# Dense experts of the second layer: product with v laid out by token rows, weighted u part stationary, two PSUM banks for u

## The chip, the cores and the metric

The program runs on one core of one Trainium2 chip. The metric is the device time of one execution in microseconds (us). Engines are called as in the profile: PE (matrix products), DVE (vector engine), ACT (scalar engine), POOL (GpSimd), SP (the engine whose queue issues most DMAs).

## The reference, cut to what matters

A two-layer backbone: each layer mixes tokens (attention, chunk MLP, Fourier), and then every token asks 8 heads x 16 experts out of 16384. Only the second half of the second layer is touched by the change:

```python
def block(t):                                            # 128 tokens
    q = rms_unit((t @ w_q).reshape(T, PEER_HEADS, 2, PEER_HALF))
    s = jnp.einsum('thpc,hpkc->thpk', q, sub_keys)
    ...                                                  # idx: 8 x 16 experts of a token, g: their softmax weights
    act = jax.nn.gelu(jnp.einsum('td,thkd->thk', t, u_tab[idx]))
    return jnp.einsum('thk,thkd->td', g * act, v_tab[idx])
x = x + mod[:, 5] * peer_ffn(h2, ...)                    # 512 latent tokens, 1024 channels
```

## The kernel before, in words

**Dense and gathered token blocks.** The 512 latent tokens are four blocks of 128. For some blocks all 16384 experts are evaluated densely and weighted by a table that is zero where a token did not choose an expert; for the others the chosen rows of u and v are gathered. `NDBS = (4, 3)`: layer 1 has four dense blocks (TD = 512 columns), layer 2 has three (TD = 384) and one gathered block.

**The dense loop.** The experts go by in 128 chunks of 128. All factors are split into a high and a low part, so a product is three matmuls (`mm3`, L111: H x H, H x L, L x H).
- The u part of a chunk (`dense_u`, L930): the chunk's u tile is loaded (wraw), split (ACT makes wH, POOL makes wL), and 24 matmuls of TD columns fill one PSUM bank (du); ACT takes it out through Gelu (gS).
- The v part (`dense_v`, L944): the v tile is loaded (vr), ACT copies its high part (vH), DVE subtracts for the low part (vL). DVE multiplies gS by the routing weights (L964); ACT and DVE split that into AH and AL (L967). Then eight blocks of 128 channels, three matmuls each, with vH or vL stationary and AH or AL (TD columns) moving. Seven blocks accumulate in seven PSUM banks over all chunks (da_0 to da_6). The eighth goes into the eighth bank (tile d7, tag "s") and DVE adds it to an array in SBUF (L980, tile da_7).
- The du tile of the dense phase has the tag "s" too, with one buffer: u parts and d7 take turns in one bank. Before the phase, beside the routing, u parts use another pool.

**What sets the order.** The loop is written chunk by chunk; `between()` (L1226) writes the next u part ahead of the v matmuls, one for each chunk that is not "spilled". u parts run ahead: 40 chunks (c % 3 == 2, c below 120) have their gS written to DRAM early and read back into gSr (L959, two buffers); 30 more stay in SBUF. So u parts end before chunk 85, and the last 43 chunks (85 to 127) have v parts alone. Each engine runs its instructions in a fixed order, which a scheduler of the programming layer chooses from the written program by its own estimate of durations. The programmer's only hold on it is `issue_after`: L963 orders the multiplication of chunk c (gS or gSr by gt) behind the addition (L980) of chunk c - 2.

**Loads.** SP issues the loads in order: vr (512 KB, three buffers), wraw (512 KB), gSr (192 KB, one in three chunks, two buffers), and gt, the routing weights of eight chunks (1536 KB, two buffers, L950). A load into a buffer waits until the last reader of the tile that held it before.

**Gathered block.** A step asks for one row per token (POOL, L838) and three steps later uses it on DVE (L857 for u, L866 for v). Steps are spread over the matmul columns by `pace`. The rows land in four buffers.

**The end.** After the last chunk DVE adds modulation and residual channel block by channel block from PSUM (L1237 to L1245). The gathered block's result is loaded as token rows and transposed on PE, four 128x128 per bank (`residual`, L876); the scheduler interleaves the two banks, and DVE reads each transposed block (L888).

Of the kernel before, what the change touches and what calls it, by code (L numbers as in the profile page):

```python
# [10 lines left out]
F32 = mybir.dt.float32  # L11
F32R = mybir.dt.float32r
# [3 lines left out]
AF = mybir.ActivationFunctionType  # L16
# [14 lines left out]
CAND = 112         # pairs of best keys that can be among the 16 best  # L31
NK = 128
NDBS = (4, 3)      # latent token blocks whose experts are evaluated densely, per layer
OBB = 3            # buffers of the one-hot rows
XB = 2             # steps of adaLN before each of the first two norms
XA = (4, 4)        # and before the loads of each of the inputs
GP = ("px", "px")  # PSUM tags of the routing-weight table
BRE = "dve"        # engines: split of the mixers' results,
YS = "dve"         # split of the merged mixers,
ADDE = "dve"       # sums of the mixers  # L40
OB = ("PADD", "AADD") # engines of the one-hot rows of four tokens, in turns
PQB = (2, 2)       # buffers of the query weights of the routing: split, and as loaded
PQC = None         # and of the context
US = ("alt", "alt") # engine that splits the expert tables beside the routing, per layer
GT = 16            # tokens per group of the routing-weight table
NCG = 8            # chunks of experts per read of that table
TILE = 1800        # ns to load a weight tile
STEPS = ((1700, 1700, 1700), (1700, 1700, 1700)) # ns between two steps of the gathered experts: mixers, dense experts
LAG = 3            # steps from a gathered product to its sum
NGSS = (16, 30)    # chunks of experts by which u runs ahead of v, per layer  # L50
SPILL = ((40, 3), (40, 3)) # chunks whose u part goes to DRAM early, one in so many, per layer
FILL = (1.0, 1.3)  # steps of u and adaLN per step of the routing
LEAD = 2           # of which so many after the routing
ADA = 6            # adaLN column groups of the next layer beside its predecessor's routing
WBUFS = ((3, 2), (3, 4)) # buffers of weight tiles: split, and as loaded, per layer
FB = (1, 2)        # buffers of the Fourier matrices, per layer
PE2 = ("alt", "dve") # engines that split the weights of the projections, per layer
PE3 = ("dve", "dve") # and of q, k and v
ME = ("alt", "pool") # engines that split the weights of the merge beside the attention, per layer
CR = 1.75          # steps of the routing of the context per step of the last merge  # L60
CR2 = 1            # and per step of the routing of the latents
GATES = (0.5, 0.6) # steps of the gates per step of the Fourier and chunk mixers, per layer
ATT = (3, 1)       # steps of the merge per step of the attention, per layer
AN = (0.1, 0.2)    # and per step of the second norm
AD = (0.25, 0.3)   # steps of adaLN per step of the Fourier and chunk mixers, per layer

# tile numbers of the packed projection weights
# [6 lines left out]
PBANKS = {"ps": 4, "px": 2, "tl": 1, "fl": 1}     # PSUM banks of the projections  # L74
RBANKS = {"ps": 3, "px": 2, "tl": 2, "fl": 1}     # and from the attention on


class Ker:
# [19 lines left out]
    def split(self, H, L, src, h="act", l="dve"):  # L98
        """src = H + L, H with float32r's significant bits, L the exact rest."""
        nc = self.nc  # L100
        if h == "act":
            nc.scalar.activation(H, src, AF.Copy)  # L102
        else:
            nc.vector.tensor_copy(H, src)
        if l == "alt":          # both in turns
            self.turn = not self.turn
            l = "dve" if self.turn else "pool"
        e = nc.vector if l == "dve" else nc.gpsimd
        e.tensor_tensor(L, src, H.bitcast(F32), op=ALU.subtract)  # L109
# [8 lines left out]
    def mm3pair(self, out, qH, qL, kH, kL, h, qs):  # L118
        """the two halves of a head's 128 rows, on the two row tiles of the array."""
# [6 lines left out]
    def hilo(self, src, l="dve", own=None):  # L126
        """a [128, 1024] weight tile from DRAM, in two float32r parts; own: (pool, buffers of the parts, and as loaded)."""
# [17 lines left out]
    def interleave(*threads, until=None):  # L145
        """emits generators in turns, each (generator, steps per turn); all, or until one ends."""
# [19 lines left out]
    def rstd(self, tmp, r, v, scale, shape, tag, bufs=1, eps=None):  # L166
        """r = (v * scale + eps) ** -0.5: Newton steps from the guess that halves the exponent."""
# [16 lines left out]
    def setup(self):  # L184
# [9 lines left out]
        self.csil = cp.tile([P, KD, 4], F32R, name="csilr")      # high parts of both vectors, then low parts  # L194
# [13 lines left out]
    def setup_rest(self):  # L208
# [7 lines left out]
        for l, v in enumerate(self.lay):  # L216
# [11 lines left out]
            nc.vector.tensor_tensor(v["lam"], e[:, 1:2], e[:, 0:1], op=ALU.subtract)     # minus lambda  # L228
# [4 lines left out]
    def ada(self, l, ccs, pool=None, e="dve", tag="tl"):  # L233
        nc = self.nc
        sm, mod = self.lay[l]["sm"], self.lay[l]["mod"]
        for cc in ccs:
# [19 lines left out]
            if cc in (3, 9):          # norm gain times (1 + scale)  # L256
# [7 lines left out]
    def sumsq(self, tmp, S, k, src, tag="nt", bufs=2):  # L264
        """adds the squares of channel block k to S."""
# [8 lines left out]
    def rms(self, tmp, S, scale, T, ps=None):  # L274
        """1 / rms of the columns of S (squares, summed over the partitions), on every partition, in PSUM."""
        return self.spread(self.rmsd(tmp, S, scale, T, ps), T, ps)

    def rmsd(self, tmp, S, scale, T, ps=None, eps=None):
        """its first half: the values as diagonal matrices of 128 columns each."""
# [17 lines left out]
    def stat(self, tmp, r, T, load):  # L297
        """r = 1 / rms of the columns."""
# [4 lines left out]
    def norm(self, tmp, l, xd, T, which, si, outs, r=None, x=None, *_):  # L303
        """outs(k) -> (H, L) for channel block k; xd: [128, 8, T] in DRAM; r: 1 / rms where known; x: xd in SBUF."""
# [23 lines left out]
    def projT(self, l, n, ss, e="pool", tag=None, own=None):  # L328
        """(h @ W)^T of each stream: 128 columns on the partitions."""
# [10 lines left out]
    def projN(self, l, n, ss, e="pool"):  # L340
        """h @ W for 512 columns of each stream, tokens on the partitions."""
# [14 lines left out]
    def qknorm(self, tmp, accs, g, rope, oH, oL):  # L356
        """accs: PSUM [128 tokens, 512]; oH, oL: [128 (m, dim), head, token]."""
# [58 lines left out]
    def softmax(self, tmp, l, h, q0, qH, qL, T, klat, kctx, ze):  # L416
        """the two softmaxes of a head for 256 queries and their difference, per 128 queries; ze: EPS for the norm."""
# [13 lines left out]
        for qb in range(2):  # L431
# [18 lines left out]
            # the difference, times the sum of the first softmax, which the norm of the result takes out again  # L450
# [8 lines left out]
    def weigh(self, tmp, h, q0, ws, att, vals, T):  # L459
        """values weighed by ws, transposed, for the 256 queries."""  # L460
# [32 lines left out]
    def qkv(self, tmp, l, ss, e="pool"):  # L493
# [5 lines left out]
        for n, w in (("k", W_K), ("q", W_Q)):  # L499
# [5 lines left out]
            # cos and signed sin, each with the norm gain of its source channel  # L505
# [886 lines left out]
```

## Time and profile before

| what | value |
|---|---|
| runs, device time | 4994.27, 5004.7, 5005.57 us (median 5004.7) |
| span of the profiled execution, first to last instruction | 4993.1 us |
| the profiled execution's own device time | not listed apart; the median run is 11.6 us above the span |
| PE busy | 4532.1 us, 91% |
| DVE busy | 3535.6 us, 71% |
| DMA, mean rate | 219 GB/s |
| dense phase of layer 2 in the trace | about 4172 to 4977 us |
| end, behind the last v matmul | 4977.8 to 4993.1 us |

Times within the trace count from the first instruction. A matmul's recorded duration overlaps its successor's, so the cadence, start to start, is what a stream of matmuls costs. The number of an instruction's source line in rows is that of the kernel before.

### The profile page before, as it was taken

What the parts mean: (1) busy time and instruction counts of PE and PEld (TensorE: products, weight loads), DVE (VectorE), ACT (ScalarE), POOL (GpSimd) and SP (SyncE); (2) the same over time, 40 slices, a digit from 0 to 9 for tenths busy, and PEclk for the clock granted to TensorE, in tenths of its full rate; (3) what the DMA queues carried; (4) which work ended last, traced back from release to release, by engine and by line L of the source; (5) the groups of instructions that cost most, each with busy time, mean ns of one, the idle gap of its engine ahead of it and who ended that gap; (6) DMA issues with size and microseconds to landing.
All of it is one profiled execution on the core that took longest, in us unless ns stands there. A gap on an engine that the chain in (4) does not pass through costs nothing.

```text
span 4993.1 us, 64879 instructions
## 1 busy us (share of the span) xinstructions
PE 4532.1 (91%) x23117; PEld 3852.4 (77%) x23117; DVE 3535.6 (71%) x6922; ACT 1995.8 (40%) x3274; POOL 2083.6 (42%) x1262
## 2 busy tenths in 40 slices
PE   7999989788788899999999989989897899999998
PEld 4887778667566688877778767767687788999998
DVE  6335585977998677766767875457559986777787
ACT  4433443232678522222222233334333783333332
POOL 2111013345656565655556421111326665555531
PEclk8999999899999999999999989999898999999999
DMA  4532345566566889988889876233535668888886
GB/s 167 178 115 65 98 128 180 165 191 197 193 232 226 290 288 318 320 281 270 280 284 304 310 256 217 94 102 110 163 97 180 214 245 293 294 293 301 300 286 232
DMA packets 447364, 1092.82 MB, mean 219 GB/s; under 512 B 37056, under 2 KB 193600, under 8 KB 439872
## 3 DMA queue, kind: packets, MB, share of 16 engines
q1 hardware_dynamic: 336448, 685.97, 42.4%
q0 software_dynamic: 110592, 402.70, 23.7%
q8 instruction: 182, 2.98, 0.2%
q14 instruction: 142, 1.16, 0.1%
HBM read 970.04 MB, written 118.49 MB: 218 GB/s over the span
## 4 chain that ended last, share of the span: by engine, by line
PE 55%; DVE 17%; issue 8%; DMA 8%; POOL 5%; ACT 3%; SPq 0%; POOLq 0%; ACTq 0%; DVEq 0%
PE du L113 6%; PE du L115 5%; PE du L114 5%; PE da L114 5%; PE da L113 5%; PE da L115 5%; PE ps L114 3%; PE ps L113 3%; PE ps L115 3%; DVE row L857 2%; POOL row L838 2%; DMA row<-in_u_dram,idxc 2%; PE px L919 2%; POOL wL L109 2%; DVE wL L109 2%
## 5 line engine op out<-in xcount | busy, mean ns | idle before, releaser
L109 POOL TENSOR_TENSOR wL<-wraw,wH 128x1024 fp32r<-128x1024 f32 x307 | 761.7, 2482 | 1197.1 <-ACT wH L102 1066.9
L102 ACT ACTIVATE wH<-wraw 128x1024 fp32r<-128x1024 f32 x556 | 586.8, 1058 | 1231.5 <-PE du L114 337.2
L113 PE MATMUL du<-dH,wH 128*128 128x512 f32 (+1 forms) x2048 | 779.9, 381 | 64.4 <-DVE da L980 46.3
L115 PE MATMUL du<-dH,wL 128*128 128x512 f32 (+1 forms) x2048 | 773.2, 378 | 49.0 <-POOL wL L109 27.4
L114 PE MATMUL du<-dL,wH 128*128 128x512 f32 (+1 forms) x2048 | 770.2, 376 | 4.1 <-DVE dL L325 4.1
L114 PE MATMUL da<-AL,vH 128*128 128x512 f32 (+1 forms) x1792 | 650.5, 363 | 3.0 <-DVE AL L109 2.9
L113 PE MATMUL da<-AH,vH 128*128 128x512 f32 (+1 forms) x1792 | 646.4, 363 | 6.0 <-ACT AH L102 6.0
L115 PE MATMUL da<-AH,vL 128*128 128x512 f32 (+1 forms) x1792 | 649.5, 362 | 0.0
L857 DVE SCALAR_TENSOR_TENSOR row<-row,hn 128x1024 f32<-128x1024 f32 x384 | 526.9, 1392 | 99.4 <-DMA row<-in_u_dram,idxc 83.6
L102 ACT ACTIVATE vH<-vr 128x1024 fp32r<-128x1024 f32 x256 | 271.7, 1062 | 772.5 <-PE da L114 559.3
L109 DVE TENSOR_TENSOR wL<-wraw,wH 128x1024 fp32r<-128x1024 f32 x249 | 336.9, 1355 | 330.7 <-ACT wH L102 316.7
L866 DVE SCALAR_TENSOR_TENSOR acc<-row,dots,acc 128x1024 f32<-128x1024 f32 x381 | 502.9, 1320 | 10.8 <-DMA row<-in_v_dram,idxc 6.9
L838 POOL DMA_INDIRECT row<-in_v_dram,idxc x256 | 336.1, 1313 | 400.5 <-DVE acc L866 325.3
L113 PEld LDWEIGHTS du<-dH,wH 128*128 128x128 f32 x2048 | 399.5, 195 | 121.1 <-DVE da L980 56.6
L115 PEld LDWEIGHTS du<-dH,wL 128*128 128x128 f32 x2048 | 398.9, 195 | 99.5 <-POOL wL L109 31.9
L838 POOL DMA_INDIRECT row<-in_u_dram,idxc x256 | 340.7, 1331 | 300.3 <-DVE row L857 203.7
L114 PEld LDWEIGHTS du<-dL,wH 128*128 128x128 f32 x2048 | 399.4, 195 | 44.5 <-DVE dL L325 5.4
L980 DVE TENSOR_TENSOR da<-d,da 128x512 f32<-128x512 f32 (+1 forms) x254 | 158.2, 623 | 328.1 <-PE d L115 327.7
L113 PEld LDWEIGHTS da<-AH,vH 128*128 128x128 f32 x1792 | 337.2, 188 | 42.2 <-ACT AH L102 7.2
L114 PEld LDWEIGHTS da<-AL,vH 128*128 128x128 f32 x1792 | 337.3, 188 | 41.1 <-DVE AL L109 6.0
L115 PEld LDWEIGHTS da<-AH,vL 128*128 128x128 f32 x1792 | 337.3, 188 | 35.1
L109 DVE TENSOR_TENSOR vL<-vr,vH 128x1024 fp32r<-128x1024 f32 x256 | 326.1, 1274 | 47.4 <-ACT vH L102 45.4
(389 smaller groups left out, 9543.7 us busy)
## 6 DMA issues: line engine op xcount, KB each, us to landing
wraw<-in_uT_dram SPq DMA_DIRECT2D x256, 512.0 KB, 4.5
vr<-in_v_dram SPq DMA_DIRECT2D x256, 512.0 KB, 6.5
wraw<-in_wt_dram SPq DMA_DIRECT2D x204, 512.0 KB, 3.8
gd<-stg SPq DMA_DIRECT2D x56, 1024.0 KB, 5.2
wraw<-in_wada_dram SPq DMA_DIRECT2D x96, 512.0 KB, 4.2
gt<-gd SPq DMA_DIRECT2D x16, 2048.0 KB, 16.8
gt<-gd SPq DMA_DIRECT2D x16, 1536.0 KB, 12.9
gatex<-g SPq DMA_DIRECT2D x48, 256.0 KB, 2.4
```

Source lines behind the costliest of these rows:

```text
L102: nc.scalar.activation(H, src, AF.Copy)
L109: e.tensor_tensor(L, src, H.bitcast(F32), op=ALU.subtract)
L113: nc.tensor.matmul(out, aH, bH, start=start, stop=False)
L114: nc.tensor.matmul(out, aH, bL, start=False, stop=False)
L115: nc.tensor.matmul(out, aL, bH, start=False, stop=stop)
L838: nc.gpsimd.indirect_dma_start(out=row, out_offset=None, in_=self.a[f"{job['tab']}{job['l']}"], in_offset=bass.IndirectOffsetOnAxis(ap=r[" ...
L857: nc.vector.scalar_tensor_tensor(row, row, 1.0, job["hn"], op0=ALU.mult, op1=ALU.mult, accum_out=dots[:, j:j + 1])
L866: nc.vector.scalar_tensor_tensor(job["acc"], row, dots[:, j:j + 1], job["acc"], op0=ALU.mult, op1=ALU.add)
L919: nc.tensor.matmul(gp[:, j * P:(j + 1) * P], ob[:, j, :], oa[:, j, :], start=True, stop=True)
L980: add = nc.vector.tensor_tensor(acc7, s[:, :TD], acc7, op=ALU.add)
```

## The change

In a layer with at most three dense blocks (`rows`, so layer 2 alone) the v product is laid out by token. For each of three token blocks and each half of 512 channels three matmuls run with AH or AL (128 tokens) stationary and vH or vL (512 columns) moving: 18 matmuls of 512 columns instead of 24 of 384. The six results fill six PSUM banks and stay there over all chunks; there is no d7 tile and no addition L980. The tag "s" gets two buffers. At the end the three blocks' sums are copied from PSUM (half by ACT, half by DVE) and pass through `residual` as the gathered block does. Nothing is put into `self.added` in this layer, so the multiplication by the routing weights has no `issue_after`. Layer 1 runs as before.

```diff
-    def residual(self, tmp, l, xin, xout, b, accd, si, nb=2):
+    def residual(self, tmp, l, xin, xout, b, accd, si, nb=2, sums=None, ps=None):
...
-        nc.sync.dma_start(acc, accd)
+        if sums is None:
+            nc.sync.dma_start(acc, accd)
+        else:
+            nc.scalar.activation(acc[:, :512], sums[0], AF.Copy)
+            nc.vector.tensor_copy(acc[:, 512:], sums[1])
...
-            tp = self.ps("tl")
+            tp = ps() if ps else self.ps("tl")
...
-    def dense_v(self, l, c, vp, sp, gS, gd, accs, acc7, between):
-        """adds a chunk's part of the result, transposed: seven blocks of 128 channels stay in PSUM."""
+    def dense_a(self, l, c, vp, gS, gd):
...
-        # not before the sum of two chunks ago, which the next u part waits for
-        with self.tc.issue_after(self.added[c - 2]) if c > 1 else nullcontext():
+
+        with self.tc.issue_after(self.added[c - 2]) if c - 2 in self.added else nullcontext():
             nc.vector.tensor_tensor(g3, g3, self.gt[:, :, c % NCG, :], op=ALU.mult)
...
+        return vH, vL, AH, AL
+
+    def dense_rows(self, l, c, vp, gS, gd, accs, between):
+
+        vH, vL, AH, AL = self.dense_a(l, c, vp, gS, gd)
+        between()
+        for b, halves in enumerate(accs):
+            ts = slice(b * P, (b + 1) * P)
+            for h, out in enumerate(halves):
+                ds = slice(h * 512, (h + 1) * 512)
+                self.mm3(out, AH[:, ts], AL[:, ts], vH[:, ds], vL[:, ds], c == 0, c == NK - 1)
...
-            acc7 = vp.tile([P, TD], F32, name=f"da{l}_7")
+            rows = TD <= 3 * P
...
-                        gSs[c] = self.dense_u(l, c, op, up, dH, dL, "s", 1)
+                        gSs[c] = self.dense_u(l, c, op, up, dH, dL, "s", 1 + rows)
...
+                for b in range(NDB if rows else 0):
+                    self.residual(vp, l, xm, xfin, b, None, 0, 3, accs[b], lambda: op.tile([P, 512], F32, tag="s", name=self.nm("s"), bufs=2))
```

On every engine the order is the same as before up to the start of the dense phase of layer 2 (but for buffer names). Three places behind that:

**PE, one v part of the last chunk.** Before, three of the eight blocks, with the one that goes to the shared bank (d7) in the middle:

```order
L113 MATMUL da1_3_34032<-AH_7659_41432,vH_7657_41427 128x384
L114 MATMUL da1_3_34032<-AL_7660_41433,vH_7657_41427 128x384
L115 MATMUL da1_3_34032<-AH_7659_41432,vL_7658_41428 128x384
L113 MATMUL d7_7661_41448<-AH_7659_41432,vH_7657_41427 128x384
L114 MATMUL d7_7661_41448<-AL_7660_41433,vH_7657_41427 128x384
L115 MATMUL d7_7661_41448<-AH_7659_41432,vL_7658_41428 128x384
```

Of the change, the first token block of the same chunk, both halves:

```order
L113 MATMUL da1_00_34028<-vH_7530_40409,AH_7532_40414 128x512
L114 MATMUL da1_00_34028<-vL_7531_40410,AH_7532_40414 128x512
L115 MATMUL da1_00_34028<-vH_7530_40409,AL_7533_40415 128x512
L113 MATMUL da1_01_34029<-vH_7530_40409,AH_7532_40414 128x512
L114 MATMUL da1_01_34029<-vL_7531_40410,AH_7532_40414 128x512
L115 MATMUL da1_01_34029<-vH_7530_40409,AL_7533_40415 128x512
```

Fewer and longer matmuls; the second matmul of a chunk now reads vL, and the third AL.

**DVE, around the spilled chunk 95, where u parts have ended.** vL and AL are the low parts that a chunk's v matmuls need, gSr the weighted u part read back from DRAM, gt the routing weights of eight chunks, acc a gathered row's use. Before (gSr_7430 is chunk 95's own, gt_7435 belongs to the next eight chunks):

```order
L964 TENSOR_TENSOR gSr_7430_40145<-gSr_7430_40145,gt_7374_39850 128x384
L109 TENSOR_TENSOR vL_7429_40142<-vr_7427_40139,vH_7428_40141 128x1024
L109 TENSOR_TENSOR AL_7432_40149<-gSr_7430_40145,AH_7431_40148 128x384
L980 TENSOR_TENSOR da1_7_34025<-d7_7425_40122,da1_7_34025 128x384
L866 SCALAR_TENSOR_TENSOR acc_6797_36600<-row_7404_40011,dots_5666_30507,acc_6797_36600 128x1024
L964 TENSOR_TENSOR gS_6957_37495<-gS_6957_37495,gt_7435_40181 128x384
L109 TENSOR_TENSOR vL_7438_40186<-vr_7436_40183,vH_7437_40185 128x1024
```

Of the change (AL_7337 is chunk 95's; gSr_7374 is chunk 101's and takes the buffer of gSr_7335; gt_7443 belongs to chunks 112 to 119):

```order
L109 TENSOR_TENSOR AL_7337_39387<-gSr_7335_39383,AH_7336_39386 128x384
L866 SCALAR_TENSOR_TENSOR acc_6760_36302<-row_7319_39310,dots_5666_30507,acc_6760_36302 128x1024
L109 TENSOR_TENSOR vL_7334_39380<-vr_7332_39377,vH_7333_39379 128x1024
L969 TENSOR_TENSOR gSr_7374_39581<-gSr_7374_39581,gt_7339_39411 128x384
L109 TENSOR_TENSOR AL_7344_39421<-gS_6906_37085,AH_7343_39420 128x384
L866 SCALAR_TENSOR_TENSOR acc_6760_36302<-row_7325_39342,dots_5666_30507,acc_6760_36302 128x1024
L109 TENSOR_TENSOR vL_7342_39416<-vr_7340_39413,vH_7341_39415 128x1024
L109 TENSOR_TENSOR AL_7350_39453<-gS_6919_37156,AH_7349_39452 128x384
L866 SCALAR_TENSOR_TENSOR acc_6760_36302<-row_7331_39371,dots_5666_30507,acc_6760_36302 128x1024
L109 TENSOR_TENSOR vL_7348_39448<-vr_7346_39445,vH_7347_39447 128x1024
L969 TENSOR_TENSOR gS_7079_38019<-gS_7079_38019,gt_7443_39940 128x384
L969 TENSOR_TENSOR gS_7098_38121<-gS_7098_38121,gt_7443_39940 128x384
```

Before, a chunk's multiplication stands right ahead of its own vL and AL, and 26 to 34 DVE rows behind the AL that frees its gSr buffer. In the change 38 gSr multiplications (chunks 8 to 119) stand 2 to 5 rows behind that AL, six chunks ahead of their use. Of the gt groups, the first multiplication stood 8 or 9 chunks behind the last reader of the buffer's earlier tile; now it stands one chunk behind it for eight groups (4 and 6 to 12) and two for five (3, 5 and 13 to 15); group 2 stands in a burst with the groups before it, at chunk 2.

**SP, the end of the program.** rx are residual tiles of a token block, racc token rows of results. Before:

```order
L882 DMA rx_7667_41488<-xm1_23471 128x8x128
L1245 DMA out_0_dram<-xr_7662_41462 128x2x384
L1245 DMA out_0_dram<-xr_7663_41467 128x2x384
L1245 DMA out_0_dram<-xr_7664_41472 128x2x384
L1239 DMA xr_7665_41477<-xm1_23471 128x2x384
L880 DMA racc_7666_41486<-accdx3_1_23477 128x1024
L1245 DMA out_0_dram<-xr_7665_41477 128x2x384
L889 DMA out_0_dram<-rx_7667_41488 1024x1x128
```

Of the change:

```order
L887 DMA rx_7535_40439<-xm1_23471 128x8x128
L887 DMA rx_7539_40463<-xm1_23471 128x8x128
L882 DMA racc_7546_40512<-accdx3_1_23477 128x1024
L894 DMA out_0_dram<-rx_7535_40439 1024x1x128
L894 DMA out_0_dram<-rx_7539_40463 1024x1x128
L887 DMA rx_7543_40487<-xm1_23471 128x8x128
L887 DMA rx_7547_40514<-xm1_23471 128x8x128
L894 DMA out_0_dram<-rx_7543_40487 1024x1x128
L894 DMA out_0_dram<-rx_7547_40514 1024x1x128
```

Four token blocks pass through `residual`, with two rx buffers: the loads of the last two stand behind the stores of the first two.

## Rows read from the trace of the kernel before

**Rows 1.** The page: span, and busy time of PE and DVE

```profile
span 4993.1 us, 64879 instructions
...
PE 4532.1 (91%) x23117; PEld 3852.4 (77%) x23117; DVE 3535.6 (71%) x6922; ACT 1995.8 (40%) x3274; POOL 2083.6 (42%) x1262
```

**Rows 2.** Stretches: length, busy time (count) per engine, PE clock, DMA

```profile
core 0: us, PE busy (x) PEld busy (x) DVE busy (x) ACT busy (x) POOL busy (x), PEclk, DMA share, GB/s
...
4205.00:4819.00 614.00, 603.25 (x3441) 598.71 (x3440) 457.40 (x575) 215.45 (x288) 341.40 (x215) 0.99 0.88 294
4819.00:4946.00 127.00, 122.96 (x698) 121.84 (x697) 112.44 (x147) 43.41 (x58) 30.60 (x27) 0.99 0.85 286
...
4211.30:4214.80 3.50, 3.44 (x11) 3.44 (x12) 3.22 (x6) 0.52 (x1) 1.78 (x2) 0.53 0.84 301
4320.70:4324.10 3.40, 3.40 (x13) 3.40 (x12) 0.89 (x2) 0.00 (x0) 1.23 (x1) 0.51 0.80 264
```

**Rows 3.** All waits of PE, 4170 to 4978: total us, times, longest

```profile
PE du L113 <- DVE da L980: 10.4, 6, 2.5
PE da L113 <- ACT AH L102: 4.0, 1, 4.0
PE du L113 <- ACT gS L939: 2.2, 1, 2.2
```

**Rows 4.** Timeline of PE, layer 2: two matmuls, 24 apart

```profile
4640.26 0.33 PE L113 MATMUL du<-dH,wH 128*128 128x384 f32 x1
...
4644.42 0.33 PE L113 MATMUL da<-AH,vH 128*128 128x384 f32 x1
```

**Rows 5.** Timeline of PE, layer 1: two matmuls, 24 apart

```profile
2103.06 0.39 PE L113 MATMUL du<-dH,wH 128*128 128x512 f32 x1
...
2108.50 0.39 PE L113 MATMUL da<-AH,vH 128*128 128x512 f32 x1
```

**Rows 6.** Timeline of DVE at a spilled chunk, layer 2

```profile
4471.06 0.55 DVE L964 TENSOR_TENSOR gSr<-gSr,gt 128x384 f32<-128x384 f32 x1
4471.53 1.22 DVE L109 TENSOR_TENSOR vL<-vr,vH 128x1024 fp32r<-128x1024 f32 x1
4472.66 0.56 DVE L109 TENSOR_TENSOR AL<-gSr,AH 128x384 fp32r<-128x384 f32 x1
```

**Rows 7.** Timeline of SP at the same chunk

```profile
4473.25 0.33 SPq L959 DMA_DIRECT2D gSr<-gsd  x1
```

**Rows 8.** DMA issues, 4205 to 4819: count, size, median us to landing

```profile
gt<-gd SPq DMA_DIRECT2D x11, 1536.0 KB, 12.9
gSr<-gsd SPq DMA_DIRECT2D x29, 192.0 KB, 7.0
```

**Rows 9.** DMA issues, 4819 to 4946

```profile
gt<-gd SPq DMA_DIRECT2D x3, 1536.0 KB, 11.5
gSr<-gsd SPq DMA_DIRECT2D x8, 192.0 KB, 5.3
```

**Rows 10.** Groups of DVE and ACT by form, 4205 to 4946: busy, mean ns, idle before

```profile
L866 DVE SCALAR_TENSOR_TENSOR acc<-row,dots,acc 128x1024 f32<-128x1024 f32 x127 | 173.2, 1364 | 3.2 <-DMA row<-in_v_dram,idxx 3.2
...
L980 DVE TENSOR_TENSOR da<-d,da 128x384 f32<-128x384 f32 x117 | 65.0, 556 | 132.7 <-PE d L115 132.7
...
L102 ACT ACTIVATE AH<-gS 128x384 fp32r<-128x384 f32 x79 | 40.9, 518 | 41.2 <-DVE gS L964 40.6
```

**Rows 11.** Who waited for the load of gt (L950), whole program

```profile
  DVE gS L964: 13.2, 1
```

**Rows 12.** Timeline of the end

```profile
4977.45 0.34 PE L115 MATMUL da<-AH,vL 128*128 128x384 f32 x1
...
4984.59 0.66 PE L887 MATMUL tl<-ident,racc 128*128 128x128 f32 x2 [6.80 <-DMA racc<-accdx]
...
4985.48 0.73 PE L887 MATMUL tl<-ident,racc 128*128 128x128 f32 x2 [0.23 <-DVE rx L888]
...
4988.48 0.56 SPq L889 DMA_DIRECT2D out_dram<-rx  x1
```

More of the change, by code (lines that the diff above doesn't have):

```diff
@@ L967, in dense_v @@
         self.split(AH, AL, gS, "act", "dve")
+        return vH, vL, AH, AL
[7 more added lines that the diff above has]
+                self.mm3(out, AH[:, ts], AL[:, ts], vH[:, ds], vL[:, ds], c == 0, c == NK - 1)
+    def dense_v(self, l, c, vp, sp, gS, gd, accs, acc7, between):
+        nc, TD = self.nc, self.TD
+        vH, vL, AH, AL = self.dense_a(l, c, vp, gS, gd)
         between()
@@ L1217, in layer @@
             vp = self.pool(e, f"dv{l}")
-            acc7 = vp.tile([P, TD], F32, name=f"da{l}_7")
+            rows = TD <= 3 * P
+            acc7 = None if rows else vp.tile([P, TD], F32, name=f"da{l}_7")
             with ExitStack() as e2:
                 op = self.pool(e2, f"dacc{l}", 1, PSUM)
-                accs = [op.tile([P, 512], F32, name=f"da{l}_{d}")[:, :TD] for d in range(KD - 1)] + [acc7]
+                if rows:
+                    accs = [[op.tile([P, 512], F32, name=f"da{l}_{b}{h}") for h in range(2)] for b in range(NDB)]
+                else:
+                    accs = [op.tile([P, 512], F32, name=f"da{l}_{d}")[:, :TD] for d in range(KD - 1)] + [acc7]
                 self.added = {}
@@ L1232, in layer @@
                     room[0] += not self.spilled(l, c)
-                    self.dense_v(l, c, vp, op, gSs[c], gd, accs, acc7, between)
+                    if rows:
+                        self.dense_rows(l, c, vp, gSs[c], gd, accs, between)
+                    else:
+                        self.dense_v(l, c, vp, op, gSs[c], gd, accs, acc7, between)
+                for b in range(NDB if rows else 0):
+                    self.residual(vp, l, xm, xfin, b, None, 0, 3, accs[b], lambda: op.tile([P, 512], F32, tag="s", name=self.nm("s"), bufs=2))
                 known = not last and TD == SEQ
@@ L1236, in layer @@
                     S = vp.tile([P, SEQ], F32, tag="gSr", name=self.nm("vS"), bufs=2)
-                for d in range(0, KD, 2):
+                for d in range(0, 0 if rows else KD, 2):
                     x = vp.tile([P, 2, TD], F32, tag="vraw", name=self.nm("xr"), bufs=3)
```

## The prediction, on record before the result was known

> **What bounds the kernel now.** I read the page first: PE is busy for 4532.1 of 4993.1 us, DVE for 3535.6 [rows 1]. Only the dense phase of layer 2 and what follows it changes, so the stretches come next: from 4205 to 4819 PE is busy for 603.25 of 614 us, and from 4819 to 4946 for 122.96 of 127, while DVE works for 112.44 of the same 127 [rows 2]. So PE sets the pace, and where only v parts are left DVE is close behind: the reader should keep those 88% in mind. The list of PE's waits says what is left to gain by waiting less: 10.4 us for the addition of the eighth block (six times), 4.0 us once for AH, 2.2 us once for a Gelu [rows 3]. The timelines give the price of a matmul in a stream, start to start: 24 matmuls of 384 columns take 4.16 us, 173.3 ns each [rows 4]; 24 of 512 columns take 5.44 us, 226.7 ns each [rows 5].
>
> **The change part by part.**
>
> *Matmuls.* A v part was 24 x 173.3 = 4.16 us and becomes 18 x 226.7 = 4.08 us [rows 4, 5]. The columns are the same (9216); six times 13.3 ns go, since 226.7 - 173.3 = 53.4 ns for 128 columns leaves 13.3 ns that do not depend on columns. Over 128 chunks: -10.2 us, all on PE. The Trainium skill (TensorE: Matmul & The Clock Gate, Back-to-back issue gap) has columns / 2.4 plus 2.5 ns; by it six matmuls fewer would save 15 ns a chunk and 1.9 us in all, and the trace disagrees, with 13.3 ns.
>
> *The shared bank.* d7 and its addition go: 128 x 0.556 us = 71 us of DVE work [rows 10], beside PE, worth nothing by itself. PE's wait for it goes: -10.4 us [rows 3], and the slow matmuls that follow two of these stalls: from 4211.3 to 4214.8 the granted clock is 0.53, the lower of the two levels, and 11 matmuls take 3.5 us in place of 1.9, and 4320.7 to 4324.1 is like it [rows 2, 4]; -3.2 for both. A Gelu no longer stands between two u parts, with two banks: -2.2 us [rows 3]. I leave the 4.0 us for AH as they are. Sum of the gains: -26.0 us.
>
> *The end.* Today 15.3 us pass from the last v matmul (4977.45 plus its cadence, 4977.8) to the end at 4993.1 [rows 1, 12]. A block's eight transposes and their readers take four rounds of 0.9 us (4984.59 to 4985.48 is one), and a store takes 4.6 us, from 4988.48 to the end [rows 12]. Now four blocks pass with two rx buffers. Counted from the last v matmul: block 0 is done at 4.2, block 1 at 8; the store of block 0 lands at 8.8 and only then block 2's residual is loaded, to 13.4 (a load priced as a store); block 2 is done at 17; block 3's residual lands at about 17.3, it is done at 21, stored at 25.6. That is +10 us. Bounds: +4 if loads take 2 us less, +14 if the copies from PSUM are late.
>
> *The order on DVE.* This decides. With nothing in `self.added`, the multiplications by gt move ahead of where they are needed, by the scheduler's own estimate of a load. A gSr load is issued the moment the AL of the earlier tile has freed its buffer: AL ends at 4473.22, SP issues at 4473.25 [rows 6, 7]. It lands 7.0 us later, or 5.3 in the late stretch; a gt load takes 12.9 or 11.5 [rows 8, 9]. Before, 26 to 34 DVE rows lay between that AL and the next use of the buffer; now 2 to 5. DVE takes its instructions in order, as the 13.2 us show that a multiplication once waited for gt [rows 11]; so vL and AL of the next chunks stand behind the load.
>
> Chunks 85 to 127, v parts alone. Let time run from the end of the v part two chunks before a spilled chunk s, which frees the buffers of AH and AL. AH takes 0.52, AL 0.56 (to 1.1), a gathered row 1.36, vL 1.22 (to 3.7) [rows 6, 10]. The gSr load issued at 1.1 lands at 6.4; the multiplication ends at 7.0. AL(s+1) 7.5, row 8.9, vL(s+1) 10.1. PE has done v(s-1) and v(s) at 8.16 and wants vL(s+1) for its second matmul, at 8.4: 1.7 us late. Ten such places (at s = 86, 89, ... 113): 17 us. Without the load in the way vL(s+1) would be there at 7.8, so this stretch has only 0.6 us to spare. Three gt groups (13 to 15) come on top: the load is issued at 7.0 and lands at 18.5, DVE gets there at 13.2, does three multiplications to 20.1 and then AL, row, vL(s+3) to 23.2; PE wants that at 18.3. Three times 4.9: 15 us. Together 32.
>
> Chunks 8 to 84, with u parts. Here PE does u, v(s-1), v(s), u, v(s+1), and vL(s+1) is wanted at 16.7: the gSr load lands at 8.1, vL(s+1) is ready at 11.7. Nothing is lost. Of the gt groups, three or two chunks' distance is enough (ready at 27.6, wanted at 29). With one chunk's distance (eight groups) DVE stands still from about 13 to 21.6; vL(s+2) comes at 25.2, wanted at 25, and after two more rows and four multiplications vL(s+3) at 32.9, wanted at 29.3. That is 0 to 3.8 us for each, by how many of the rows and multiplications lie there; I take half, 1.9, eight times: 15.
>
> Bounds of this term: 0 (nothing reaches PE) to 30 + 32 = 62 us, and half as much again in the late stretch if rows land later, 78. I take 32 + 15 = 47.
>
> The Trainium skill (DMA: Bandwidth & Descriptors, Latency and other measured facts) puts the fixed cost of a DMA at about 2 us. By it a gSr load would be there before DVE asks for it at 3.7, and the gSr places would cost nothing; the trace disagrees, 5.3 to 7.0 us [rows 8, 9].
>
> *Sum.* -26 + 10 + 47 = +31 us on the profiled execution, 5024 in its span. The runs' median lies 11.6 us above the span, for what surrounds it, which the change doesn't touch: 5004.7 + 31 = 5036.
>
> *Without price.* PE's transposes in the end (24 more) lie in the rounds above. POOL's requests for rows wait for DVE as before; its weight splits stand behind them, and a DVE stall of 9 us may delay a wL: cover is the second wL buffer, one u part ahead.
>
> **The rivals.**
>
> *The loads are hidden (faster or same).* If the scheduler's early multiplications cost PE nothing, -26 + 10 = -16 remain: 4989. For it: with u parts the gSr places have 5 us to spare, DVE loses 71 us of work, and DVE sat idle for 132.7 us waiting for d7 [rows 10], time that can be spent waiting for loads as well. Against: the v-only stretch has 0.6 us to spare by my count, and loads land there in 5.3 us, not in 3.
>
> *DVE becomes the bound (much slower).* From 4205 to 4946 DVE works for 570 us, less 65 for additions: 505 [rows 2, 10]. 28 places of 3.4 us (7.0 less the 3.6 until DVE asks), ten of 2.7, and 13 gt groups of some 6 are 200 us more: 705 of the 715 that PE needs. Whether they fit depends on when they come; if half of them meets a PE that has nothing to do, 100 us are lost: 5004.7 - 16 + 100 = 5089. Against: vL and AL are made one to two chunks ahead.
>
> *The end costs all.* The other terms cancel, and the longer end alone shows: within 15 us of before.
>
> **How the numbers follow.** My forecast (late stretch bound by loads, slower by 16 to 60 us) has 0.52; loads hidden 0.28 (0.2 of it beyond 0.3% faster, the rest inside); DVE as bound 0.08; about even 0.12. A measurement of this kernel can tell about 0.3%, 15 us, from no change. So: faster 0.21, same 0.2, slower 0.59. The range reaches from just under the hidden case, 4985, to 5072, which takes in the bounds of the DVE term and leaves most of the last rival out; the forecast's own range is 5020 to 5065.
>
> **What would show it.** Right: the waits of PE name DVE vL or AL, not the addition; gS and gSr multiplications on DVE have idle time ahead of them, ended by DMA gt or gSr, some 150 us in all; between the ends of the v parts of the last 43 chunks PE stands still for 1 to 3 us every third chunk; v matmuls come at 227 ns; the end takes about 25 us. Wrong: PE as busy as before in the late stretch with a phase about 25 us shorter (the loads were hidden), or PE waiting for wL or wraw (POOL was the one to look at), or v matmuls at another cadence than 227 ns.

## The result, and the profile after

The changed kernel takes 5034.56 us (median of 4 runs, 5023.99 to 5041.2), the kernel before, run beside it, 4999.49 us. The ratio is 1.0062, 95% interval 1.0049 to 1.0076: slower by 25 to 38 us.

Spans can't be subtracted to see where this arose: the profiled execution of before (span 4993.1) was shorter than the median run, and the code ahead of the dense phase, which is the same, takes some 20 us more or less from one execution to the next (the last matmul of the routing-weight table, px, comes at 4127.0 before, at 4138.7 after, and between 4119.5 and 4141.3 in the other kernels below). So all stages here are counted from that px matmul, to the last v matmul and to the end:

| kernel | px to last v matmul | last v matmul to end | px to end |
|---|---|---|---|
| before | 850.4 | 15.7 | 866.1 |
| after | 867.9 | 27.8 | 895.7 |
| after, multiplications held (first experiment) | 825.0 | 26.8 | 851.8 |

By stages the change costs 29.6 us: 17.5 in the product, 12.1 behind it. The first experiment splits the 17.5 into a gain of 25.4 and a loss of 42.9. How far such stages repeat: two kernels of the sixth experiment, whose instructions stand in the first experiment's order up to the last v matmul but for loads of the end, take 827.0 us each for its 825.0, and one that stands so to the changed kernel takes 872.0 for 867.9. Single profiles, then, are good to some 2 to 4 us.

The page of after, span and busy time, answers to [rows 1]:

```profile
span 5034.4 us, 63461 instructions
...
PE 4543.0 (90%) x22373; PEld 3765.2 (75%) x22373; DVE 3500.6 (70%) x6813; ACT 1989.2 (40%) x3277; POOL 2138.2 (42%) x1262
```

The two stretches of [rows 2], and two short ones behind a stall (length, busy time and count of each engine, granted PE clock, DMA share, GB/s):

```profile
4205.00:4819.00 614.00, 593.96 (x2888) 526.40 (x2888) 431.84 (x479) 205.94 (x283) 371.59 (x213) 0.99 0.84 288
4819.00:4946.00 127.00, 112.75 (x477) 90.70 (x476) 90.35 (x108) 39.02 (x53) 47.85 (x29) 0.97 0.80 275
...
4443.60:4447.20 3.60, 3.60 (x9) 2.83 (x10) 2.41 (x5) 0.00 (x0) 0.00 (x0) 0.50 0.89 283
4874.80:4878.40 3.60, 3.60 (x9) 2.83 (x10) 3.39 (x6) 0.00 (x0) 1.21 (x1) 0.50 0.70 226
```

PE has fallen from 603.25 to 593.96 of 614 us and from 122.96 to 112.75 of 127. DVE is less busy too, 90.35 for 112.44: neither engine is full, so something stands between them. The five longest sums of PE's waits from 4130 on name it (total us, times, longest), beside [rows 3]:

```profile
PE da L114 <- DVE vL L109: 34.1, 15, 6.4
PE s L892 <- DVE rx L893: 10.0, 11, 6.7
PE du L115 <- POOL wL L109: 7.3, 4, 3.5
PE du L115 <- DVE wL L109: 1.4, 1, 1.4
PE du L113 <- ACT gS L944: 1.4, 1, 1.4
```

The addition and AH are gone from the list; vL has come, fifteen times. And what DVE itself waits for, 4180 to 5020, the three longest sums:

```profile
DVE gSr L969 <- DMA gSr<-gsd: 113.0, 37, 9.0
DVE AL L109 <- ACT AH L102: 70.0, 40, 4.2
DVE gS L969 <- DMA gt<-gd: 53.1, 12, 8.0
```

166 us of DVE's time pass ahead of a multiplication whose operand is still on its way. The longest stall of PE shows how that reaches it. DVE first, with its idle time in brackets:

```profile
4428.57 0.56 DVE L969 TENSOR_TENSOR gS<-gS,gt 128x384 f32<-128x384 f32 x1 [7.93 <-DMA gt<-gd]
...
4434.09 7.82 DVE L969 TENSOR_TENSOR gS<-gS,gt 128x384 f32<-128x384 f32 x5
4441.84 0.55 DVE L109 TENSOR_TENSOR AL<-gSr,AH 128x384 fp32r<-128x384 f32 x1
4442.30 1.21 DVE L109 TENSOR_TENSOR vL<-vr,vH 128x1024 fp32r<-128x1024 f32 x1
```

and PE beside it:

```profile
4436.74 0.39 PE L113 MATMUL da<-vH,AH 128*128 128x512 f32 x1
4443.57 0.80 PE L114 MATMUL da<-vL,AH 128*128 128x512 f32 x1 [6.44 <-DVE vL L109]
4444.16 0.63 PE L115 MATMUL da<-vH,AL 128*128 128x512 f32 x1
```

DVE stands 7.93 us for gt, works off what has piled up, among it five more multiplications that nobody needs yet, and only then makes the vL that the second matmul of the chunk reads. The other stalls are like it in this: ahead of each of the fifteen, within 16 us, stands a wait of DVE for gt or gSr. Behind the stall PE runs at the lower clock (0.50 in the third stretch above): matmuls of 0.63 us for 0.39.

### The profile page after: what moved, and what is told of

It reads as the page before. It is cut to its first block, busy times and chain, and to the rows that moved or that the text cites. A ratio compares the mean times of both kernels' runs of the same rounds, so it can differ in the third digit from the quotient of the medians.

```text
span 5034.4 us, 63461 instructions
## 1 busy us (share of the span) xinstructions
PE 4543.0 (90%) x22373; PEld 3765.2 (75%) x22373; DVE 3500.6 (70%) x6813; ACT 1989.2 (40%) x3277; POOL 2138.2 (42%) x1262
## 4 chain that ended last, share of the span: by engine, by line
PE 52%; DVE 17%; DMA 9%; issue 8%; POOL 5%; ACT 3%; SPq 0%; POOLq 0%; DVEq 0%; ACTq 0%
PE du L113 5%; PE du L115 5%; PE du L114 5%; PE da L114 5%; PE da L115 5%; PE da L113 5%; PE ps L114 3%; PE ps L113 3%; PE ps L115 3%; DMA row<-in_u_dram,idxc 2%; POOL wL L109 2%; PE px L924 2%; DVE row L857 2%; POOL row L838 2%; PE px L113 1%
## 5 line engine op out<-in xcount | busy, mean ns | idle before, releaser
L109 POOL TENSOR_TENSOR wL<-wraw,wH 128x1024 fp32r<-128x1024 f32 x307 | 772.2, 2517 | 1152.7 <-ACT wH L102 1032.8
L857 DVE SCALAR_TENSOR_TENSOR row<-row,hn 128x1024 f32<-128x1024 f32 x384 | 512.9, 1355 | 103.5 <-DMA row<-in_u_dram,idxc 89.9
L114 PE MATMUL da<-AL,vH 128*128 128x512 f32 x896 | 349.7, 390 | 1.8 <-DVE AL L109 1.7
L115 PE MATMUL da<-AH,vL 128*128 128x512 f32 x896 | 349.4, 390 | 0.0
L113 PE MATMUL da<-AH,vH 128*128 128x512 f32 x896 | 347.1, 390 | 2.1 <-ACT AH L102 2.1
L924 PE MATMUL px<-oa,ob 128*128 128x128 f32 x1792 | 268.0, 292 | 86.6 <-DVE oa L913 22.9
L924 PEld LDWEIGHTS px<-oa,ob 128*128 128x128 f32 x1792 | 236.4, 198 | 140.5 <-ACT ob L919 49.8
L114 PE MATMUL da<-vL,AH 128*128 128x512 f32 x768 | 305.1, 397 | 34.3 <-DVE vL L109 34.1
L115 PE MATMUL da<-vH,AL 128*128 128x512 f32 x768 | 302.9, 394 | 0.0
```

The costliest lines, as they stand in the source:

```text
L113: nc.tensor.matmul(out, aH, bH, start=start, stop=False)
L114: nc.tensor.matmul(out, aH, bL, start=False, stop=False)
L115: nc.tensor.matmul(out, aL, bH, start=False, stop=stop)
L857: nc.vector.scalar_tensor_tensor(row, row, 1.0, job["hn"], op0=ALU.mult, op1=ALU.mult, accum_out=dots[:, j:j + 1])
L924: nc.tensor.matmul(gp[:, j * P:(j + 1) * P], ob[:, j, :], oa[:, j, :], start=True, stop=True)
```

## The experiments

Each ratio is to runs of the kernel before made beside it, with its 95% interval; stages are from the profiled execution.

**1. The hold put back.** In layer 2 the multiplication of chunk c comes behind the low-part split (AL) of chunk c - 2, as it came behind the addition before.

```diff
...
-        self.split(AH, AL, gS, "act", "dve")
+        low = self.split(AH, AL, gS, "act", "dve")
+        if rows:
+            self.added[c] = low.ins
...
-        vH, vL, AH, AL = self.dense_a(l, c, vp, gS, gd)
+        vH, vL, AH, AL = self.dense_a(l, c, vp, gS, gd, True)
```

> The change, with each multiplication by gt in layer 2 ordered behind the AL of two chunks ago. Theory (the early multiplications stall DVE and through vL PE): DVE's waits for gSr and gt, 166 us in the changed kernel, fall below 10; PE's 34 us for vL fall below 6; the time falls by 35 to 45 us, to 4990 to 5000 (0.998 to 1.000 of before), since the longer end stays. Rival (the layout itself: the second matmul of a chunk now reads vL, so vL comes too late whatever the order): PE still waits 20 us or more for vL, and the time stays above 5020.

Measured: 4993.29 us, ratio 0.9971 (0.9958 to 0.9984). PE's three longest sums of waits, 4130 to the end, the two stretches, and DVE's longest sum:

```profile
PE s L892 <- DVE rx L893: 9.4, 11, 6.2
PE du L115 <- POOL wL L109: 7.2, 3, 3.5
PE da L114 <- DVE vL L109: 1.7, 3, 0.8
```

```profile
4205.00:4819.00 614.00, 614.00 (x3014) 547.23 (x3013) 400.13 (x505) 215.17 (x295) 376.51 (x220) 1.00 0.88 301
4819.00:4946.00 127.00, 124.15 (x545) 101.59 (x544) 98.77 (x120) 44.81 (x60) 41.40 (x25) 1.00 0.84 282
```

```profile
DVE AL L109 <- ACT AH L102: 250.9, 88, 12.2
```

PE is busy throughout the first stretch at full clock; the wait for vL falls from 34.1 to 1.7 us, so the new layout alone doesn't make vL late, and DVE's waits for gSr and gt are gone. DVE still waits, 250.9 us for AH, and that costs nothing: what it waits for matters, not how long. The kernels have the same instructions, and PE and ACT the same order; DVE's differs, and with it that of some loads on SP and of the weight splits among the row requests on POOL. With this order the product is 42.9 us shorter than in the changed kernel.

**2. The early multiplications in the kernel before.** The same test from the other side: only the hold of layer 2 is taken away, the old product stays.

```diff
-        with self.tc.issue_after(self.added[c - 2]) if c > 1 else nullcontext():
+        with self.tc.issue_after(self.added[c - 2]) if c > 1 and l == 0 else nullcontext():
```

> The kernel before, without the order of the multiplications in layer 2, and nothing else changed. Theory: the scheduler moves gSr's multiplication 1 to 9 rows behind the AL that frees its buffer here too, DVE waits for gSr and gt some 150 us, and PE waits on DVE; since d7's addition stands behind these multiplications as well, it is worse than in the changed kernel: 30 to 80 us slower than before. Rival (only the new layout suffers from that order): within 10 us of before.

Measured: 5091.91 us, ratio 1.018 (1.0159 to 1.0201), 90 us slower. PE's three longest sums of waits, 4165 to 5080:

```profile
PE du L113 <- DVE da L980: 54.0, 31, 6.5
PE d L113 <- DVE da L980: 19.0, 15, 2.1
PE da L114 <- DVE AL L109: 7.3, 8, 3.5
```

The direction holds, the size is over what was expected. In the old layout a late DVE meets PE at the addition, which must empty the one shared bank, 73 us in 46 waits; the new layout has no such place, and pays less for a like order.

**3. Which load.** Two kernels hold one kind of multiplication each and leave the other free: first those of parts kept in SBUF are held (so gSr is early, gt isn't), then those of parts read back (gt early, gSr not). Against experiment 1:

```diff
-        with self.tc.issue_after(self.added[c - 2]) if c - 2 in self.added else nullcontext():
+        with self.tc.issue_after(self.added[c - 2]) if c - 2 in self.added and (l == 0 or not self.spilled(l, c)) else nullcontext():
```

```diff
-        with self.tc.issue_after(self.added[c - 2]) if c - 2 in self.added else nullcontext():
+        with self.tc.issue_after(self.added[c - 2]) if c - 2 in self.added and (l == 0 or self.spilled(l, c)) else nullcontext():
```

> The changed kernel in which, in layer 2, the multiplications of parts kept in SBUF are held behind the split of two chunks before, and those of the parts read back from DRAM (gSr) are left free. On VectorE a gSr multiplication then still stands 3 or 4 rows behind the split that frees its buffer, while the multiplications by a new gt stand 6 to 9 chunks behind the last reader of the gt buffer. The part of the loss that is left is what the early gSr multiplications cost. Prediction's term: 17 us of the 47, in the late stretch; with it the time is 4993 + 17, 5005 to 5018 us, and VectorE waits about 100 us for gSr and under 10 for gt. Rival: the gSr waits are hidden and only the gt groups cost: within 5 us of the first experiment, 4988 to 4998 us, with the same waits on VectorE.

> The mirror image: the gSr multiplications are held (they stand 16 to 30 rows behind the split that frees their buffer), those of the parts kept in SBUF are free, so the first multiplication by a new gt stands one or two chunks behind the last reader of its buffer. What is left is the cost of the gt groups. Prediction's term: 30 us of the 47 (15 beside u parts, 15 in the late stretch), 5015 to 5028 us, with VectorE waiting 50 us or more for gt and under 10 for gSr. Rival: a gt group costs only where gSr waits have used up the slack already; alone it costs under 10 us: 4993 to 5003 us.

Measured, gSr early: 5007.02 us, ratio 1.0018 (1.0003 to 1.0032); px to end 873.9, 22.1 more than with both held. The stretch with u parts (to 4778) and the one behind it:

```profile
4205.00:4778.00 573.00, 572.12 (x2823) 511.56 (x2822) 400.31 (x468) 201.30 (x277) 354.57 (x210) 1.00 0.88 303
4778.00:4946.00 168.00, 151.48 (x632) 122.27 (x631) 115.63 (x137) 51.19 (x70) 50.97 (x32) 0.96 0.77 257
```

and PE's wait:

```profile
PE da L114 <- DVE vL L109: 15.8, 9, 3.5
```

Where u parts run, the early gSr costs nothing (572.12 of 573 us busy, though DVE waits 144.9 us for gSr in all); where v parts are alone it costs what was expected. On POOL the order is that of experiment 1 here, and on SP a few loads alone have moved, so these 22.1 us are the early gSr's on DVE.

Measured, gt early: 5049.14 us, ratio 1.0106 (1.0082 to 1.013); px to end 916.9, 65.1 more than with both held. PE's wait and DVE's:

```profile
PE da L114 <- DVE vL L109: 47.6, 14, 6.7
```

```profile
DVE AL L109 <- ACT AH L102: 168.1, 64, 11.3
DVE gS L969 <- DMA gt<-gd: 118.6, 14, 11.3
```

Both theories miss: every gt group costs PE some 3.4 us of waits (47.6 by 14), ten of the fourteen while u parts still run. And the two parts don't add: 22.1 and 65.1 make 87, the changed kernel loses 43.9 with both. DVE waits 118.6 us for gt here and 53.1 there, perhaps because, waiting for gSr on the way, it comes to the gt multiplication later. The order differs as well: the first multiplication by a new gt stands one chunk behind the last reader of the buffer in 11 groups here, in 8 there. How much each of the two does was not taken apart.

**4. More buffers instead of a hold.** gSr gets four buffers in layer 2.

```diff
-            gS = vp.tile([P, TD], F32, tag="gSr", name=self.nm("gSr"), bufs=2)
+            gS = vp.tile([P, TD], F32, tag="gSr", name=self.nm("gSr"), bufs=2 if l == 0 else 4)
```

> The changed kernel with four instead of two buffers for the spilled u parts that are read back in layer 2 (192 KB each, 5 to 7 us to land). Theory (order): what costs time is that VectorE's instructions stand in an order in which a multiplication that waits for a load is ahead of the split that TensorE needs; more buffers let the multiplication be placed still earlier, so the waits stay. VectorE still waits over 90 us for gSr (113.0 us in the changed kernel), TensorE still waits over 25 us for vL, and the time is within 10 us of the changed kernel's, 5025 to 5045 us. Rival (too few buffers): the load is issued late only because its buffer comes free late; with four it is there when VectorE comes to it, the gSr wait falls below 50 us, TensorE's wait for vL below 15, and the time to 5000 to 5015 us.

Measured: 5022.44 us, ratio 1.0045 (1.0032 to 1.0058); DVE's and PE's waits:

```profile
DVE gSr L969 <- DMA gSr<-gsd: 94.3, 35, 6.5
```

```profile
PE da L114 <- DVE vL L109: 28.2, 13, 6.0
```

By the waits the order theory holds; the time is just under the range that was expected and some 9 us below the changed kernel's (ratios 1.0045 and 1.0062, whose intervals overlap). With four buffers the multiplication stands 2 to 4 rows behind the split that frees the fourth one back, as it did behind the second one: the scheduler uses up what room it is given. The test is a narrow one: the gt multiplications stay free, on which most of the loss beside u parts hangs. More buffers for gt were not tried.

**5. The second bank for u.** Experiment 1 with one bank.

```diff
...
-                        gSs[c] = self.dense_u(l, c, op, up, dH, dL, "s", 1 + rows)
+                        gSs[c] = self.dense_u(l, c, op, up, dH, dL, "s", 1)
...
-                    self.residual(vp, l, xm, xfin, b, None, 0, 3, accs[b], lambda: op.tile([P, 512], F32, tag="s", name=self.nm("s"), bufs=2))
+                    self.residual(vp, l, xm, xfin, b, None, 0, 3, accs[b], lambda: op.tile([P, 512], F32, tag="s", name=self.nm("s")))
```

> The kernel of the first experiment (the changed one with each multiplication in layer 2 held behind the split of two chunks before) with one PSUM bank for the u product and for the final transposes instead of two. Theory: nothing but u writes that bank now, and 18 matmuls of 227 ns (4.1 us) of the v product lie between two u parts, longer than the Gelu that empties the bank; one bank costs 0 to 4 us in the product and some us at the end, where the transposes take turns with VectorE in one bank: 4994 to 5003 us, with under 6 us of TensorE waits for the Gelu. Rival: the second bank is what removed the 10.4 us wait of the kernel before, and without it that wait comes back: over 10 us of TensorE waits at the first u matmul, 5004 to 5012 us.

Measured: 4990.19 us, ratio 0.9978 (0.9965 to 0.9991), not to be told from experiment 1. px to the last v matmul is 823.8 us (825.0 with two banks); the end takes 32.7 for 26.8. PE's three longest sums of waits:

```profile
PE s L892 <- DVE rx L893: 12.1, 23, 1.6
PE du L115 <- POOL wL L109: 3.8, 2, 3.5
PE du L113 <- ACT gS L944: 2.7, 2, 1.4
```

In the product the second bank is worth nothing that these profiles show: the waits that the change removed at the shared bank went because d7 left it. The second bank lets two more u parts run ahead of the first v part, and for these PE waits 3.4 us more for wL.

**6. The end.** First the residual tiles of the third and fourth block go into vL's two buffers, so that their loads needn't wait for the stores; then the same with the hold; then that with the four transposes of a bank ahead of the four multiply-adds.

```diff
...
-        x = tmp.tile([P, D], F32, tag="vH", name=self.nm("rx"), bufs=2).rearrange("p (k t) -> p k t", t=P)
+        x = tmp.tile([P, D], F32, tag=xtag, name=self.nm("rx"), bufs=2).rearrange("p (k t) -> p k t", t=P)
...
-                    self.residual(vp, l, xm, xfin, b, rx[b]["accd"], 0, 3)
+                    self.residual(vp, l, xm, xfin, b, rx[b]["accd"], 0, 3, None, None, "vL")
```

```diff
...
                 nc.tensor.transpose(tp[:, j * P:(j + 1) * P], acc[:, k * P:(k + 1) * P], self.ident)
+            for j in range(4):
+                k = 4 * q + j
                 nc.vector.scalar_tensor_tensor(x[:, k, :], ...
...
```

> The change, with the residual tiles of the third and fourth block in the two buffers of vL, so that their loads no longer wait for the stores of the first two. Theory (the end costs 12 us because of two rx buffers): the end, last v matmul to end of span, falls from 27.8 to 17 to 20 us; the time falls by 8 to 11, to about 5025. Rival (the end is bound by four blocks of transposes and their readers): less than 4 us gained.

> Both edits. Theory: the two add up, 45 to 55 us off the changed kernel, 4980 to 4990, 0.995 to 0.998 of before: what the product laid out by rows and the second bank were worth by the sum (26 us) less a rest of the longer end. Rival (early multiplications and end overlap, or the layout gains nothing): not below before by more than 5 us.

> The kernel of the third experiment (hold, and residual tiles of the third and fourth block in the vL buffers) with the four transposes of a bank all ahead of the four multiply-adds that read them, instead of one after the other. Theory: what is left of the end (22.8 us from the last v matmul to the end) is 16 rounds of 0.92 us in which TensorE and VectorE wait for each other in one bank, of which VectorE is busy 0.61; in groups of four the two banks overlap, the rounds fall to 0.61 to 0.75 us per pair, the end to 18 to 20 us and the time by 3 to 5 us, to 4978 to 4981 us. Rival: the residual's loads (512 KB each, four in a row on one queue) and the last store set the end; the rounds get shorter but wait for the loads, the end stays above 21.5 us and the time within 1 us of 4983.

Measured: with the buffers alone 5026.69 us, ratio 1.0048 (1.0033 to 1.0063), end 23.0; with the hold 4982.81, ratio 0.996 (0.9945 to 0.9975), end 22.8; with the transposes first 4981.47, ratio 0.9961 (0.9947 to 0.9974), end 19.6. The buffers brought 5 us of the end instead of the 8 to 11 expected, since sixteen rounds of two multiply-adds, most of them 0.92 us, are left. With the hold the two gains add up, as expected. DVE in the end of the second kernel:

```profile
4961.46 0.61 DVE L893 SCALAR_TENSOR_TENSOR rx<-s,mod,rx 128x128 f32<-128x128 f32 x2 [0.31 <-PE s L892]
4962.38 0.61 DVE L893 SCALAR_TENSOR_TENSOR rx<-s,mod,rx 128x128 f32<-128x128 f32 x2 [0.31 <-PE s L892]
```

and of the third:

```profile
4963.10 2.16 DVE L895 SCALAR_TENSOR_TENSOR rx<-s,mod,rx 128x128 f32<-128x128 f32 x8 [2.08 <-DMA rx<-xm]
4965.49 2.16 DVE L895 SCALAR_TENSOR_TENSOR rx<-s,mod,rx 128x128 f32<-128x128 f32 x8 [0.23 <-PE s L892]
```

Two multiply-adds per 0.92 us became eight per 2.4 us. The end is 3.2 us shorter by the trace, and the time by no amount that these runs can tell. All four kernels with both multiplications held (this one, the one before it, and those of experiments 1 and 5) beat the kernel before, by 0.2 to 0.4%, with intervals below 1.

## Why the prediction was right

**Matmuls, -10.2 us: right.** A v part of after, 18 matmuls from start to start, takes 4.08 us, as [rows 5] had it:

```profile
4643.04 0.39 PE L113 MATMUL da<-vH,AH 128*128 128x512 f32 x1
...
4647.12 0.39 PE L113 MATMUL da<-vH,AH 128*128 128x512 f32 x1
```

The formula of the Trainium skill (TensorE: Matmul & The Clock Gate, Back-to-back issue gap) that the prediction sets against its 13.3 ns is given there for an isolated matmul, not for a stream of weight loads and matmuls as here (22373 of each, by the page of the profile), so the trace doesn't contradict it.

**Shared bank, clock and Gelu, -15.8 us; with the matmuls -26: right as a sum, with errors that cancel.** With the hold back, px to the last v matmul is 25.4 us shorter than before. The addition's wait is gone. The 4.0 us for AH, which the prediction left in, went too. The slow matmuls were undercounted: summed over the starts between 4205 and 4946 that come late without a wait, they cost some 8 us before, not 3.2, and 0.3 in experiment 1. Against these gains stands one loss that was missing: from 4130 on PE waits some 7 us for wL (7.2 in experiment 1, 7.3 in the changed kernel), with two more u parts ahead of the first v part. Before, from 4130 on:

```profile
PE du L115 <- POOL wL L109: 3.8, 2, 3.5
```

Experiment 5, where it is 3.8 again, shows that this comes with the second bank.

**The end, +10 us: right, +12.1.** The place is the one named, the third block's residual, loaded only behind a store (the stores of the first two blocks were issued from 5010.65 on):

```profile
5015.55 3.90 SPq L887 DMA_DIRECT2D rx<-xm  x2
...
5021.75 0.61 DVE L893 SCALAR_TENSOR_TENSOR rx<-s,mod,rx 128x128 f32<-128x128 f32 x2 [6.85 <-DMA rx<-xm]
```

It isn't the whole of it: with loads that needn't wait for stores the end is still 7.3 us longer than before (23.0 for 15.7, experiment 6), for the rounds of three more blocks, which the prediction's count has too.

**The order on DVE, +47 us: right in kind, and in size by luck.** It cost 42.9. DVE's waits for gSr and gt were 166 us (150 were said), PE's wait was for vL, as said. The parts are another matter. Here they are, counted from the px matmul to the last u matmul and from there to the last v matmul, each against experiment 1 (645.6 and 179.5 us):

| part | predicted | measured |
|---|---|---|
| early gSr, beside u parts | 0 | 0.9 (alone) |
| early gSr, late stretch | 17 | 21.0 (alone) |
| early gt, beside u parts | 15 | 46.0 (alone) |
| early gt, late stretch | 15 | 18.9 (alone) |
| both, beside u parts | 15 | 27.7 |
| both, late stretch | 32 | 15.2 |

Three of the four single terms hold. The fourth, gt beside u parts, was three times too small: one chunk's distance was priced at half of 0 to 3.8 us, and eight groups were to have it; alone, eleven groups had it, and the ten that reached PE in this stretch cost 4.6 us each. Against that the prediction added the two loads, and they don't add: together they cost 43, alone 22 and 65. The two errors cancel, and that is luck; in the changed kernel the loss lies beside u parts for the greater part, not in the late stretch, where PE stood still seven times and not every third chunk.

Two things were left out of the price of a stall. Each long stall is followed by slow matmuls: summed over the starts that come late between 4205 and 4946, matmuls of after took 46.5 us beyond their cadence (3.9 in experiment 1), of which waits are 34.1. And DVE works off its backlog more slowly than it was charged (last section).

**From the sum to the time: two slips.** The 11.6 us "around the span" are not there: the profiled execution of after took 5036.62 us with a span of 5034.4, so 2.2. By that, the rest of the 11.6 was that the profiled execution of before was shorter than the median run. And the median it was added to, 5004.7 us of three runs, falls to 4999.49 with a fourth. So the forecast of 5036 stood on a difference of +31, where the medians differ by 35.1 and the stages of the two profiles by 29.6; that it came within 2 us of 5034.56 is luck.

**The rivals.** That the loads are hidden fell with experiment 1: 42.9 us hang on the order alone. It is true of the gSr loads beside u parts where they are early alone (0.9 us), as the prediction reckoned. DVE was never the bound: it is 71% busy in the late stretch (90.35 of 127). Nor did the end cost all: 17.5 of the 29.6 us arose in the product, where gain and loss did not cancel.

## What to carry to other kernels

Where a scheduler sets the order, look at what a removed instruction was holding back: here an addition that cost PE 10.4 us of waits was the anchor of the loads' users, and without one the users moved up until they waited for their own loads, at the head of an engine that takes its work in order. Put such an anchor on something that stays; four buffers for two did not replace it here. Compare stages from a common point of the trace, not spans, when the code ahead of the change varies by more than the change is worth.

## What the runs showed that was not expected

A DVE instruction can take six times its usual time beside one of POOL. A multiplication of 128x384 takes 0.55 us; the second of the five in the stall above:

```profile
4434.56 3.26 DVE L969 TENSOR_TENSOR gS<-gS,gt 128x384 f32<-128x384 f32 x1
```

and POOL at that time:

```profile
4435.00 2.39 POOL L109 TENSOR_TENSOR wL<-wraw,wH 128x1024 fp32r<-128x1024 f32 x1
```

It ends 0.43 us after POOL's subtraction does. Its like behave so too: the DVE instructions of after that took over 1.3 times the median of their kind (35 between 4205 and 4946) all lie beside a wL. Two of the five in that stall took 5.4 us more than usual together; PE's stall is 6.44. Summed over such instructions, DVE loses 64 us in after, 32 before and 11 in experiment 1. The Trainium skill (SBUF — State Buffer, SBUF: two separate sides) says that VectorE with two inputs in SBUF and a GpSimd operation that reads SBUF take a shared pair of ports by an exclusive lock, whichever starts first, for the whole instruction; the length agrees, 3.26 us for 0.55, while on which started first the records say nothing clear (DVE's row starts 0.44 us ahead of POOL's, and DVE is the one that is late). Why the multiplications of a DVE that comes out of a wait meet POOL more often wasn't tried, nor how much of PE's loss goes with it; that POOL's work and DVE's are the same in experiment 1 and meet less shows that it goes with the order on the two.

In the changed kernel the loads themselves land sooner than in [rows 8]. DMA issues, 4205 to 4819 (count, size, median us to landing):

```profile
gt<-gd SPq DMA_DIRECT2D x10, 1536.0 KB, 9.2
gSr<-gsd SPq DMA_DIRECT2D x29, 192.0 KB, 4.3
```

9.2 for 12.9 us and 4.3 for 7.0, with a DMA share of 0.84 for 0.88. In the late stretch it is 8.1 for 11.5 and 4.8 for 5.3 [rows 9]. So the durations of before on which the DVE term stood were too long for the changed kernel, least so for gSr in the late stretch, which its 17 us stood on; why they fell was not tried.
